# One weight group loaded in four transfers of one row k each, in place of one transfer

## The chip, the cores and the metric

The kernel runs on one core of one Trainium2 chip. The metric is the time of the kernel on the device in microseconds (us), as a median over runs. The profile comes from one execution; its span is counted from the first instruction that the profile shows, so it is a little shorter than the time.

## The reference

The kernel computes a bilinear form for 32 pairs of vectors and 128 weight matrices:

```python
batch, dim_i, dim_j, dim_k = 32, 256, 256, 128
x: [batch, dim_i] float32
y: [batch, dim_j] float32
weight: [dim_k, dim_i, dim_j] float32       # 33.6 MB

out[b, k] = sum over i, j of x[b, i] * y[b, j] * weight[k, i, j]
```

The weight is nearly all of the data. Each row k of it is a matrix of 256 x 256 float32, which is 256 KiB in one piece.

## The kernel before

The 128 rows k are taken in 32 groups of 4 rows: group g holds k = g, g+32, g+64 and g+96. On chip, partition p = 4 * ip + kk holds eight neighbouring i (i = 8 * ip to 8 * ip + 7) of row k = 32 * kk + g, so each partition receives 8 KiB of contiguous weight per group. The PE multiplies a group by a matrix that holds x in the right places, adding up over the eight i, and the DVE multiplies the sums by y and adds over j.

Thirty of the groups are brought in by transfers on the Pool queue, which turn float32 into bf16 on the way. The first two groups to be issued (0 and 16) are brought in as float32 by the SP and ACT queues, and ACT turns them into bf16 with copies. These are the parts concerned:

```python
UNITS = (                         # groups that share a stretch of PE and DVE work
    tuple(range(0, 32, 2)), tuple(range(1, 32, 4)), (3, 11, 19, 27), (7, 23), (15,), (31,),
)
LOADS = (                         # transfers on the Pool queue: groups, from ic, to ic
    ((8, 24), 0, 8), ((4, 12, 20, 28), 0, 8), (tuple(range(2, 32, 4)), 0, 8),
    (tuple(range(1, 32, 4)), 0, 8), ((3, 11, 19, 27), 0, 8), ((7, 23), 0, 8), ((15,), 0, 8),
    ((31,), 0, 4), ((31,), 4, 6), ((31,), 6, 7), ((31,), 7, 8),
)
FIRST = (0, 16)                   # the two float32 groups
# ...
    def rows_of(groups):
        step = G // len(groups)
        v = weight.rearrange("(u s) (ip ic) j -> s ip u (ic j)", s=step, ic=IC)
        return v[groups[0]]       # one group: 32 ip x 4 kk x 2048 elements
# ...
    w_sb = sbuf("w_sb", [P, G, IC * J], bf16)
    w_f = sbuf("w_f", [P, len(FIRST), IC * J], f32)
# ...
    sw = [nc.gpsimd.dma_start(out=w_of(groups)[:, :, lo * J:hi * J],
                              in_=rows_of(groups)[:, :, lo * J:hi * J]).then_inc(s, 16).ins
          for (groups, lo, hi), s in zip(LOADS, s_w)]
    # ... the load of y is put in as the third of these
    hw = [nc.scalar.dma_start(out=x_sb, in_=x).then_inc(s_x, 16).ins]
    for n, (g, queue) in enumerate(zip(FIRST, (nc.sync, nc.scalar))):
        hw.append(queue.dma_start(
            out=w_f[:, n:n + 1, :], in_=rows_of((g,)),
        ).then_inc(s_f[n], 16).ins)
    # ... both lists are moved ahead of the barrier that starts the program
    for n, g in enumerate(FIRST):
        for h in range(2):
            lo, hi = h * IC * J // 2, (h + 1) * IC * J // 2
            c = act.copy(out=w_sb[:, place_of[g], lo:hi], in_=w_f[:, n, lo:hi])
            if h == 0:
                c._wait_ge(s_f[n], 16)
            c.then_inc(s_act, 1)
# ...
    pe.wait_ge(s_act, 2 * len(FIRST))
    pe.wait_ge(s_dve, t_x)
    # ... then per unit: products (each waits for its load), DVE multiply and sum
    sp.dma_start(out=out_v, in_=acc)._wait_ge(s_dve, n_dve).then_inc(s_out, 16)
```

Of the kernel before, what the change touches and what calls it, by code (L numbers as in the profile page):

```python
# [31 lines left out]
FIRST = (0, 16)  # L32
# [4 lines left out]
def kernel(  # L37
# [7 lines left out]
    nc = tc.nc  # L45
# [10 lines left out]
    KK = P // B  # L56
    IP = P // KK
    IC = I // IP
    G = K // KK
# [6 lines left out]
    def sbuf(name, shape, dtype):  # L66
        return nc.alloc_sbuf_tensor(name, shape, dtype).ap()

    def rows_of(groups):


        step = G // len(groups)
        assert all(g == groups[0] + n * step for n, g in enumerate(groups))
        v = weight.rearrange("(u s) (ip ic) j -> s ip u (ic j)", s=step, ic=IC)
        return v[groups[0]]

    def w_of(groups):
        at = [place_of[g] for g in groups]
        step = at[1] - at[0] if len(at) > 1 else 1
        assert all(a == at[0] + n * step for n, a in enumerate(at))  # L80
        return w_sb[:, at[0]:at[-1] + 1:step, :]

    w_sb = sbuf("w_sb", [P, G, IC * J], bf16)
    w_f = sbuf("w_f", [P, len(FIRST), IC * J], f32)
# [18 lines left out]
        for s, (groups, lo, hi) in zip(s_w, LOADS) for g in groups for ic in range(lo, hi)  # L103
    }
    s_f = [nc.alloc_semaphore(f"f{g}") for g in FIRST]
# [15 lines left out]
            out=w_of(groups)[:, :, lo * J:hi * J],  # L121
            in_=rows_of(groups)[:, :, lo * J:hi * J],
# [6 lines left out]
    hw = [  # L129
        nc.scalar.dma_start(out=x_sb, in_=x).then_inc(s_x, 16).ins,  # L130
    ]
    for n, (g, queue) in enumerate(zip(FIRST, (nc.sync, nc.scalar))):
        hw.append(
            queue.dma_start(
                out=w_f[:, n:n + 1, :], in_=rows_of((g,)),
            ).then_inc(s_f[n], 16).ins
        )
    for ins in [*hw, *sw]:
        tc.no_tile_sem_insts.add(ins.name)

# [8 lines left out]
    for blk in blocks:  # L149
# [20 lines left out]
        out=ident, in_=ident, compare_op=mybir.AluOpType.not_equal, fill=1.0,  # L170
# [4 lines left out]
    for n, g in enumerate(FIRST):  # L175
        for h in range(2):
            lo, hi = h * IC * J // 2, (h + 1) * IC * J // 2
            c = act.copy(out=w_sb[:, place_of[g], lo:hi], in_=w_f[:, n, lo:hi])  # L178
            if h == 0:
                c._wait_ge(s_f[n], 16)  # L180
            c.then_inc(s_act, 1)


# [2 lines left out]
    def done(ins):  # L186
# [6 lines left out]
        out=x_rep,  # L193
        in_=x_sb.rearrange("b (ip ic) -> b ic ip", ic=IC).unsqueeze(3)
        .to_broadcast([B, IC, IP, KK]),
    )._wait_ge(s_x, 16))
    for q in range(Q):
        c = v.transpose(  # L198
            out=xt[q * 32:(q + 1) * 32, :, :],
            in_=x_rep[:, :, q * IP // Q:(q + 1) * IP // Q, :],  # L200
        )
# [4 lines left out]
        out=mask, in_=ident.rearrange("p (ip kk) -> p kk ip", kk=KK), axis=AX, op=add,  # L206
    )._wait_ge(s_pool, 2))

    for kk in range(KK):
        c = v.tensor_scalar(  # L210
            out=xblk[:, :, :, kk], in0=xt, scalar1=mask[:, kk:kk + 1],
            scalar2=None, op0=mult,
        )
# [6 lines left out]
        out=yt, in_=y_sb.rearrange("b (jb j) -> b jb j", j=32),  # L220
    )._wait_ge(s_y, 16))
    t = done(v.tensor_copy(  # L222
        out=y_rep, in_=yt.unsqueeze(3).to_broadcast([B, J // 32, B, KK]),
    )._wait_ge(s_dve, t))
    BQ = B // Q
    for q in range(Q):
        c = v.transpose(  # L227
            out=y4[q * 32:(q + 1) * 32, :].rearrange("p (jb j) -> p jb j", j=32),
            in_=y_rep[:, :, q * BQ:(q + 1) * BQ, :],
        )  # L230
# [5 lines left out]
    def product(out, lhsT, rhs, first, last, load):  # L236
        return pe.add_instruction(mybir.InstMatmult(  # L237
            name=nc.get_next_instruction_name(), engine=mybir.EngineType.PE,
            ins=[pe.lower_ap(rhs), pe.lower_ap(lhsT)], outs=[pe.lower_ap(out)],
            start_tensor_calc=first, stop_tensor_calc=last,  # L240
            tile_size=(P, P), tile_position=(0, 0), ldweights=load,
        ))
# [9 lines left out]
    for u, unit in enumerate(UNITS):  # L252
# [13 lines left out]
        for n_step, (ic, h) in enumerate(steps):  # L266
            n = n_g // n_b
# [7 lines left out]
            for s in need[:-1]:  # L275
                pe.wait_ge(s, 16)
            c = product(
                ps[:, bank + h, :n, :],
                xblk[:, ic, :, :].rearrange("p b kk -> p (b kk)"),
                w_sb[:, p0 + o:p0 + o + n, ic * J:(ic + 1) * J],  # L280
                first=(ic == order[0]), last=(ic == order[-1]), load=(held != ic),
            )
# [10 lines left out]
        if n_g > 1:  # L293
            t = done(v.tensor_tensor(  # L294
                out=prod, in0=sums, in1=y4.unsqueeze(1).to_broadcast([P, n_g, J]), op=mult,
# [3 lines left out]
                out=acc[:, unit[0]:unit[-1] + 1:unit[1] - unit[0]], in_=prod, axis=AX, op=add,  # L299
            )._wait_ge(s_dve, t))  # L300
        else:
            done(v.tensor_tensor_reduce(  # L302
                out=prod[:, 0, :], in0=sums[:, 0, :], in1=y4, scale=1.0, scalar=0.0,
# [44 lines left out]
```

## Time and profile before

| | |
|---|---|
| time, median of 3 runs | 84.87 us (84.86 to 84.88) |
| span of the profile | 83.4 us |
| PE busy | 32.5 us (39%) |
| DVE busy | 25.2 us (30%) |
| Pool busy | 8.8 us (11%) |
| ACT busy | 5.2 us (6%) |
| read from HBM | 33.62 MB |
| Pool queue's transfers, share of the 16 DMA engines' span | 94.4% |
| the two other queues' transfers | 3.5% and 3.3% |

The shares of the engines are averages over the whole span. A low share says only that an engine has idle time, not that it is free when it matters. The profile shows the DMA both as issues (an instruction on SP, ACT or Pool that starts a transfer) and as the packets that the 16 DMA engines then move; an issue ends long before its data has landed. The page counts moved bytes as they are written, so a transfer that turns float32 into bf16 counts half of what it reads.

### The profile page before, as it was taken

To read this page: it belongs to the slowest core of one execution; us is meant where nothing else is said; L and a number is where in the kernel's file an instruction comes from. 1 tells how busy PE (TensorE), PEld (TensorE's weight loads), DVE (VectorE), ACT (ScalarE), POOL (GpSimd) and SP (SyncE) were. 2 spreads that over 40 slices of the span, in tenths; PEclk is the share of its full clock that TensorE was granted. 3 is DMA by queue.
4 is the path that set the end of the run, shared out by engine and by line. 5 is a ranking of instruction groups with operands and counts; after the bars stand their busy time and mean duration, and the time that the engine had idled before them with its cause. 6 is when DMAs were issued, how large, how long until landed. Compare 5 with 4: busy or idle time off the path is not lost.

```text
span 83.4 us, 257 instructions
## 1 busy us (share of the span) xinstructions
PE 32.5 (39%) x136; PEld 4.3 (5%) x43; DVE 25.2 (30%) x28; ACT 5.2 (6%) x5; POOL 8.8 (11%) x18
## 2 busy tenths in 40 slices
PE   0000000000000000000099999996029999884780
PEld 0000000000000000000000000000000110112330
DVE  0009450000292000000000000003999800999932
ACT  0019930000000000000000000000000000000000
POOL 5999600000000000000000000000000000000000
PEclk9999999999999999999999999999995799999998
DMA  4999999999999999999999999999999999999980
GB/s 122 393 370 293 214 214 212 216 218 212 218 218 216 212 216 216 212 218 214 212 214 218 210 220 214 214 214 216 212 214 218 212 214 216 212 216 214 197 118 8
DMA packets 4912, 17.91 MB, mean 215 GB/s; under 512 B 384, under 2 KB 800, under 8 KB 4656
## 3 DMA queue, kind: packets, MB, share of 16 engines
q0 software_dynamic: 4432, 15.76, 94.4%
q1 hardware_dynamic: 288, 1.07, 3.5%
q10 hardware_dynamic: 192, 1.08, 3.3%
HBM read 33.62 MB, written 0.02 MB: 403 GB/s over the span
## 4 chain that ended last, share of the span: by engine, by line
DMA 46%; PE 39%; DVE 6%; POOL 3%; another core or an unknown queue 3%; issue 2%; POOLq 0%
DMA w_sb<-in_weight_dram 46%; PE ps L237 39%; DVE tmp L294 5%; POOL w_sb L120 2%; POOL y_sb L127 1%; DVE tmp L302 1%; POOL const-float32-0.0 L332 0%; POOLq L332 0%; POOL const-uint8-127 L332 0%; POOL const-float32-1.0 L332 0%; DVE acc L302 0%
## 5 line engine op out<-in xcount | busy, mean ns | idle before, releaser
L237 PE MATMUL ps<-w_sb,xblk 128*128 128x512 bf16 (+1 forms) x136 | 32.5, 396 | 48.9 <-DMA w_sb<-in_weight_dram 44.2
L294 DVE TENSOR_TENSOR tmp<-ps,y 128x4096 f32<-128x4096 f32 (+3 forms) x4 | 8.6, 2156 | 36.7 <-PE ps L237 36.6
L298 DVE TENSOR_REDUCE acc<-tmp 128x16 f32<-128x4096 f32 (+3 forms) x4 | 8.6, 2154 | 0.1
L237 PEld LDWEIGHTS ps<-w_sb,xblk 128*128 128x128 bf16 x43 | 4.3, 101 | 76.9 <-DMA w_sb<-in_weight_dram 42.7
L120 POOL DMA_DIRECT2D w_sb<-in_weight_dram x11 | 7.6, 707 | 0.6 <-issue 0.6
L178 ACT CAST w_sb<-w_f 128x1024 bf16<-128x1024 f32 x4 | 3.9, 1040 | 0.0
L219 DVE STREAM_TRANSPOSE yt<-y_sb 32x256 f32<-32x256 f32 x1 | 0.4, 433 | 10.9 <-DMA y_sb<-in_y_dram 10.9
L192 DVE COPY x_rep<-x_sb 32x1024 f32<-32x1024 f32 x1 | 0.8, 790 | 6.1 <-PEq L332 6.1
L227 DVE STREAM_TRANSPOSE y<-y_rep 32x256 f32<-32x256 f32 x4 | 1.7, 435 | 0.1
L198 DVE STREAM_TRANSPOSE xt<-x_rep 32x256 f32<-32x256 f32 x4 | 1.7, 435 | 0.1
L178 ACT ACT_TABLE_LOAD x1 | 1.3, 1283 | 6.0 <-PEq L332 6.0
L210 DVE TENSOR_SCALAR xblk<-xt,mask 128x256 bf16<-128x256 f32 x4 | 1.4, 499 | 0.0
L302 DVE CUSTOM_DVE_ANT_0 tmp<-ps,y 128x256 f32<-128x256 f32 x2 | 0.8, 424 | 1.6 <-PE ps L237 1.6
L222 DVE COPY y_rep<-yt 32x1024 f32<-32x1024 f32 x1 | 0.7, 682 | 0.0
L205 DVE TENSOR_REDUCE mask<-ident 128x4 f32<-128x128 f32 x1 | 0.4, 382 | 1.0 <-POOL ident L169 1.0
L127 POOL DMA_DIRECT2D y_sb<-in_y_dram x1 | 0.5, 534 | 0.0
L168 POOL MEMSET ident<- 128x128 f32 x1 | 0.3, 302 | 0.0
L169 POOL TENSOR_SCALAR_AFFINE_SELECT ident<-ident 128x128 f32<-128x128 f32 x1 | 0.3, 287 | 0.1
L302 DVE DVE_READ_ACCUMULATOR2_ANT acc<- 128x1 f32 x2 | 0.2, 84 | 0.0
L332 POOL MEMSET const-float32-0.0<- 128x1 f32 x1 | 0.1, 98 | 0.2 <-issue 0.2
L332 POOL MEMSET const-bfloat16-1.0<- 128x1 bf16 x1 | 0.1, 101 | 0.0
L332 POOL MEMSET const-uint8-127<- 128x1 uint8 x1 | 0.1, 101 | 0.0
(1 smaller groups left out, 0.1 us busy)
## 6 DMA issues: line engine op xcount, KB each, us to landing
w_sb<-in_weight_dram POOLq DMA_DIRECT2D x2, 4096.0 KB, 48.0
w_sb<-in_weight_dram POOLq DMA_DIRECT2D x2, 2048.0 KB, 43.3
w_sb<-in_weight_dram POOLq DMA_DIRECT2D x2, 1024.0 KB, 40.9
w_f<-in_weight_dram SPq DMA_DIRECT2D x1, 1024.0 KB, 4.9
w_f<-in_weight_dram ACTq DMA_DIRECT2D x1, 1024.0 KB, 8.3
w_sb<-in_weight_dram POOLq DMA_DIRECT2D x1, 512.0 KB, 72.1
w_sb<-in_weight_dram POOLq DMA_DIRECT2D x1, 256.0 KB, 72.7
w_sb<-in_weight_dram POOLq DMA_DIRECT2D x1, 128.0 KB, 72.9
```

Source lines behind the costliest of these rows:

```text
L120: nc.gpsimd.dma_start(out=w_of(groups)[:, :, lo * J:hi * J], in_=rows_of(groups)[:, :, lo * J:hi * J],).then_inc(s, 16).ins
L127: sw.insert(2, nc.gpsimd.dma_start(out=y_sb, in_=y).then_inc(s_y, 16).ins)
L178: c = act.copy(out=w_sb[:, place_of[g], lo:hi], in_=w_f[:, n, lo:hi])
L192: t = done(v.tensor_copy(out=x_rep, in_=x_sb.rearrange("b (ip ic) -> b ic ip", ic=IC).unsqueeze(3) .to_broadcast([B, IC, IP, KK]),)._wait_ ...
L198: c = v.transpose(out=xt[q * 32:(q + 1) * 32, :, :], in_=x_rep[:, :, q * IP // Q:(q + 1) * IP // Q, :],)
L210: c = v.tensor_scalar(out=xblk[:, :, :, kk], in0=xt, scalar1=mask[:, kk:kk + 1], scalar2=None, op0=mult,)
L222: t = done(v.tensor_copy(out=y_rep, in_=yt.unsqueeze(3).to_broadcast([B, J // 32, B, KK]),)._wait_ge(s_dve, t))
L227: c = v.transpose(out=y4[q * 32:(q + 1) * 32, :].rearrange("p (jb j) -> p jb j", j=32), in_=y_rep[:, :, q * BQ:(q + 1) * BQ, :],)
L237: return pe.add_instruction(mybir.InstMatmult(name=nc.get_next_instruction_name(), engine=mybir.EngineType.PE, ins=[pe.lower_ap(rhs), pe.l ...
L294: t = done(v.tensor_tensor(out=prod, in0=sums, in1=y4.unsqueeze(1).to_broadcast([P, n_g, J]), op=mult,)._wait_ge(s_pe, n_pe))
L298: done(v.tensor_reduce(out=acc[:, unit[0]:unit[-1] + 1:unit[1] - unit[0]], in_=prod, axis=AX, op=add,)._wait_ge(s_dve, t))
L302: done(v.tensor_tensor_reduce(out=prod[:, 0, :], in0=sums[:, 0, :], in1=y4, scale=1.0, scalar=0.0, op0=mult, op1=add, accum_out=acc[:, uni ...
```

## The change

Group 0, the first float32 group, was one transfer on the SP queue that fills all 128 partitions, with four 8 KiB pieces that lie 8 MiB apart in the weight following each other. It becomes four transfers on the same queue, one for each row k. Each of them reads one row k, 256 contiguous KiB, and writes it to 32 partitions that are four apart (kk, kk+4, ...). All four count on the same semaphore, so the first copy on ACT waits for 64 instead of 16. Group 16, on the ACT queue, stays one transfer. The aim is that a short transfer can begin to move data sooner than a long one, and that each transfer reads the weight in one piece. The contents of `w_f` are the same.

```diff
-    for n, (g, queue) in enumerate(zip(FIRST, (nc.sync, nc.scalar))):
+
+    for kk in range(KK):
         hw.append(
-            queue.dma_start(
-                out=w_f[:, n:n + 1, :], in_=rows_of((g,)),
-            ).then_inc(s_f[n], 16).ins
+            nc.sync.dma_start(
+                out=w_f[kk::KK, 0, :],
+                in_=weight[kk * G + FIRST[0]].rearrange("(ip ic) j -> ip (ic j)", ic=IC),
+            ).then_inc(s_f[0], 16).ins
         )
+    hw.append(
+        nc.scalar.dma_start(
+            out=w_f[:, 1:2, :], in_=rows_of(FIRST[1:]),
+        ).then_inc(s_f[1], 16).ins
+    )
...
-                c._wait_ge(s_f[n], 16)
+                c._wait_ge(s_f[n], 16 if n else 16 * KK)
```

## The prediction

> **What bounds the kernel now.** I read the slices of the page first, then the waits of the PE, then the last stretch of the timeline, and last the start of the timeline, because only the start is touched by the change.
>
> The slices show which resource is full over the whole span. The two DMA rows of the page are:
>
> ```profile
> DMA  4999999999999999999999999999999999999980
> GB/s 122 393 370 293 214 214 212 216 218 212 218 218 216 212 216 216 212 218 214 212 214 218 210 220 214 214 214 216 212 214 218 212 214 216 212 216 214 197 118 8
> ```
>
> From the second slice to the 38th (2.1 to some 79 us) the 16 DMA engines are never idle. The rate row has two levels. Near 400 GB/s the float32 groups move (8 KiB read, 8 KiB written). Near 214 GB/s the groups that are turned into bf16 on the way move (8 KiB read, 4 KiB written); the page counts the written bytes, so the read rate there is also about 430 GB/s. The page's HBM line gives 33.62 MB read. The stream is one unbroken queue of reads.
>
> The waits of the PE (engine, line, what it waited for: us in total, times, longest) show who is ahead of whom:
>
> ```profile
> PE ps L237 <- DMA w_sb<-in_weight_dram: 44.2, 5, 41.9
> PE ps L237 <- DVE tmp L294: 4.6, 1, 4.6
> ```
>
> The PE starts its first product only at 41.87 us, when the load of 8 groups has come in. The 4.6 us behind the DVE lie at 57.5 to 62.1 us and are made good later, as the end of the timeline shows (start us, us, engine, line, what; idle before, and who ended it):
>
> ```profile
> 76.09 1.89 PE L237 MATMUL ps<-w_sb,xblk 128*128 128x512 bf16 x8 [1.32 <-DMA w_sb<-in_weight_dram]
> ...
> 78.51 1.03 PE L237 MATMUL ps<-w_sb,xblk 128*128 128x256 bf16 x8 [0.53 <-DMA w_sb<-in_weight_dram]
> ...
> 79.76 1.64 PE L237 MATMUL ps<-w_sb,xblk 128*128 128x256 bf16 x8 [0.22 <-DMA w_sb<-in_weight_dram]
> ...
> 81.44 0.42 DVE L302 CUSTOM_DVE_ANT_0 tmp<-ps,y 128x256 f32<-128x256 f32 x1 [1.42 <-PE ps L237]
> ...
> 81.90 0.35 SPq L311 DMA_DIRECT2D out_dram<-acc  x1
> ```
>
> Each of the last units waits for its load. By the trace's landing times the last load is complete at 81.07 us; one product (0.3), one product-and-sum on the DVE (0.42) and the output transfer follow, to 83.4. So the end is: start of the DMA stream, plus the time that the busiest of the 16 engines needs for its share, plus a fixed tail of 2.3 us. Only the first two can move.
>
> The start of the timeline, for the three transfers that begin the stream and the one that follows them on the Pool queue:
>
> ```profile
> 0.00 0.63 SPq L134 DMA_DIRECT2D w_f<-in_weight_dram  x1
> 0.12 0.42 ACTq L130 DMA_DIRECT2D x_sb<-in_x_dram  x1
> ...
> 0.58 0.56 ACTq L134 DMA_DIRECT2D w_f<-in_weight_dram  x1
> 1.05 1.60 POOL L120 DMA_DIRECT2D w_sb<-in_weight_dram  x2 [0.61 <-issue]
> ...
> 7.33 3.88 ACT L178 CAST w_sb<-w_f 128x1024 bf16<-128x1024 f32 x4
> ```
>
> Two things count. The issue of 128 rows took 0.63 us, that of 32 rows (x) 0.42. And the copies of the first float32 group begin at 7.33 us, while that group landed 4.9 us after its issue (page, DMA issues): ACT is held by the barrier (6.04 us) and its table load (1.28 us), not by this transfer.
>
> From the trace's packet records I take three more numbers. The first packet of x starts at 1.16 us, 1.04 us after its issue. The first packet of the first group starts at 1.42 us, 1.42 us after its issue, though issued earlier. A packet of 8 KiB takes 309 ns (26.5 GB/s per engine), except in the first round, where it takes 0.4 to 0.6 us. The group runs to 4.57 us; the second float32 group starts at 4.19 us, when the first one drains, and the casting loads from 5.48 us. No engine has a gap between these.
>
> [...] all three queues together move some 400 GB/s at the start, as one stream[...]. [...] the trace shows x (32 rows) with 16 completions. [...] No run of this case shows port contention so far. [...]
>
> **The change part by part.** Removed: one issue on SP of 128 rows by 8 KiB (0.63 us). Added: four issues on SP of 32 rows by 8 KiB. The wait of the first ACT copy goes from 16 to 64 counts, all of them needed, so it still means that all four rows k are in. Nothing else moves: the order of instructions on PE, DVE, ACT and Pool is the same.
>
> Bytes: 1 MiB before and after, 128 packets of 8 KiB, 8 per engine. Data time is 8 x 0.309 = 2.47 us per engine in both. Completions: four per engine instead of one, of 9 ns each (size of the four-byte packets in the trace), so 3 x 9 = 27 ns more per engine. On the path: +0.03 us.
>
> SP's time: by x's 0.42 us per 32-row issue and some 0.04 us between, 4 x 0.46 = 1.84 us instead of 0.63. SP then waits for the barrier until 5.96 us, which Pool releases at 5.92 us. There are 4 us of slack, so this costs nothing.
>
> Feeding: a piece of 256 KiB occupies the engines for 2 x 0.309 = 0.62 us, and the next one is issued 0.46 us later (0.67 us if each costs as much as 128 rows did). The first round is slow (0.5 to 0.6 us), which gives some 0.25 us of lead, and from about 2 us the second float32 group, issued by ACT at 0.58 us, can fill a gap. I count no gap.
>
> Start: if a 32-row transfer starts as soon after issue as x did, the stream starts at 1.04 instead of 1.42 us, up to 0.38 us earlier. Whether the 0.38 us depends on the number of rows is not shown, as x's start may also be quick for another reason (its rows are 1 KiB). I take half of it: -0.2 us. It passes to the end in full, because the engines are never idle afterwards.
>
> ACT copies: the ACT group may now slip in between the second and third piece, which puts the landing of the first group at 6 to 8 us instead of 4.9. The copies would begin perhaps 1 us after 7.33 us. They end at 11.2 us, and the PE has its first work at 41.87 us: some 30 us of slack, no cost.
>
> Sum: -0.2 + 0.03 = about -0.17 us without contention, 84.7 us.
>
> **The rivals.** First, write ports. [...] a piece could take up to twice its 0.62 us: 4 x 0.62 = 2.5 us more in the worst case, 87.2 us. [...] Against it: the starts of the engines are staggered by up to 0.26 us, which takes part of the conflict away; the second group and then the casting loads mix in[...]. I give a full conflict 6%, a partial one (+0.4 to +1.5 us) 15%.
>
> Second, the start gains nothing or the pieces leave gaps. The wait before 1.42 us may be a fixed cost of the first issue on SP, and each piece may bring its own start, with the slow first round paid again in part. For it: first-round packets cost up to 0.3 us above the later ones. That gives 0 to +0.5 us, 84.9 to 85.4. I give it 30%.
>
> Third, all of the start is gained, and 256 contiguous KiB are also read with a quicker first round. The group took 4.57 - 1.42 = 3.15 us where 2.47 are pure data, so up to 0.5 us could be had: 84.2 to 84.4. Against it: from the second round on the packets are already at 309 ns. 15%.
>
> Fourth, the issue time on SP delays the barrier. It would need SP to be busy past 5.9 us, three times what I count, and even then the DMA stream would not notice. No cost.
>
> **Range and chances.** The centre lies between the sum without contention (84.7) and the rival of ports and gaps, so 84.75 us. Below, 84.3 holds the gain of the whole start and a little of the first round. Above, 85.7 holds the gaps and a mild conflict. A gain of 2% is 1.7 us, more than the whole time from the first issue to the first packet (1.42 us); 1% for it. A loss of 2% (above 86.57 us) needs a nearly full port conflict: 7%. Within 2%: 92%.
>
> **What would show each step right or wrong.** In the profile after: four SP issues of 0.4 to 0.5 us each, done before 2 us; DMA busy by 1.1 to 1.3 us; the second slice at 390 GB/s or more; the last units still waiting on their loads, shifted by the same amount as the first landing of the casting loads (12.45 us before); the PE's first product at about 41.7 us. A second or third slice well below 370 GB/s with packets of the first group longer than 0.4 us would show the port conflict; a hole in the DMA share between 2 and 4 us would show gaps. I am wrong in kind if the shift of the end differs from that of the casting stream, since then something other than the start of the stream moved.

## The result, and the profile after

The changed kernel takes 87.17 us (86.49 to 87.67, six executions) against 84.85 us before: a ratio of 1.0276, with a 95% interval of 1.0232 to 1.032. It is slower by 2.3 us, where the prediction had 84.75 us and a range that ended at 85.7. A ratio in this document leaves out every execution more than 1.5% above the fastest of its kernel.

The order of reading is that of the prediction. First the two DMA rows of the page after, in 40 slices of 2.1 us:

```profile
DMA  3999999999999999999999999999999999999800
GB/s 119 351 326 296 231 216 220 216 216 214 217 215 216 214 218 218 216 214 216 214 214 221 214 216 214 214 216 214 214 216 214 214 218 212 216 214 200 132 10 8
```

The second and third slices moved 351 and 326 GB/s, where the kernel before had 393 and 370; the fourth, with 296, is no lower than before (293). The casting loads (those on the Pool queue that turn float32 into bf16) keep their 214 GB/s; there is only more of them at the end. The loss lies in the first 6 us.

The waits of the PE (engine, line, what it waited for: us in total, times, longest) and the end of the timeline say the same from the other side:

```profile
PE ps L244 <- DMA w_sb<-in_weight_dram: 46.8, 5, 44.3
PE ps L244 <- DVE tmp L301: 4.6, 1, 4.6
```

```profile
83.89 0.42 DVE L309 CUSTOM_DVE_ANT_0 tmp<-ps,y 128x256 f32<-128x256 f32 x1 [1.41 <-PE ps L244]
84.24 0.08 DVE L309 DVE_READ_ACCUMULATOR2_ANT acc<- 128x1 f32 x1
84.35 0.35 SPq L318 DMA_DIRECT2D out_dram<-acc  x1
```

The PE starts at 44.3 us instead of 41.9. The wait behind the DVE is the same 4.6 us, and the last product-and-sum starts at 83.89 instead of 81.44. What waits for a complete load is later by 2.4 us from first to last.

The issues of the changed kernel on SP and ACT (start, us, engine, line, what):

```profile
0.00 2.44 SPq L135 DMA_DIRECT2D w_f<-in_weight_dram  x4
```

```profile
0.12 0.40 ACTq L130 DMA_DIRECT2D x_sb<-in_x_dram  x1
0.56 0.71 ACTq L141 DMA_DIRECT2D w_f<-in_weight_dram  x1
```

Four issues of 256 KiB take 2.44 us, about 0.61 us each with the gap, where one issue of 1 MiB took 0.63. A quarter of the rows costs nearly the full issue. And a piece keeps the engines busy for 2 x 0.309 = 0.62 us. So the pieces are issued just as fast as they are moved, and I infer that no store of work builds up in front of the engines.

The stretches from 2 to 4 us show what that does. The last two columns are the share of DMA time in which a packet was under way, and the rate. Before and after:

```profile
2.00:3.00 1.00, 0.00 (x0) 0.00 (x0) 0.00 (x0) 0.00 (x0) 1.00 (x2) 1.00 1.04 426
3.00:4.00 1.00, 0.00 (x0) 0.00 (x0) 0.00 (x0) 0.00 (x0) 1.00 (x2) 1.00 0.99 401
```

```profile
2.00:3.00 1.00, 0.00 (x0) 0.00 (x0) 0.00 (x0) 0.00 (x0) 1.00 (x2) 1.00 0.91 279
3.00:4.00 1.00, 0.00 (x0) 0.00 (x0) 0.00 (x0) 0.00 (x0) 1.00 (x2) 1.00 0.96 385
```

The share falls little, the rate from 426 to 279 GB/s. So the engines are not only idle; some packets also take longer. In the trace's packet records of the changed kernel, seven of the second piece's first packets take 578 to 742 ns in place of 309. Two of the seven (694 and 731 ns) came to an engine that had been empty for some 0.5 us, the other five followed directly on the packet before. One engine is hit hardest. The records carry no engine number, but packets of one engine follow each other to within 20 ns, so its row can be put together:

```
start us   what                           took ns
2.41       group 0 (SP), 8 KiB            578
2.98       group 0 (SP), 8 KiB            332
3.31       completion of the second piece
           (nothing for 0.85 us)
4.17       group 16 (ACT), 8 KiB          1909
6.07       casting load (Pool)            489
```

The other fifteen engines got their first packet of group 16 between 3.07 and 3.55 us. This one got it at 4.17 us, empty by then, and the packet took 1.9 us. It has done one packet in 2.8 us where its neighbours did eight or nine. The trace has 16 landings for each transfer (304 for the 19 of this run), by the order of the packets one per engine. The PE goes on after the last of them: the last load's last landing is at 83.53 us, and the weight load for the product that waits for it starts at 83.57. So the slowest engine decides. The 16 landings of the last load, from the trace:

| last load lands, us | first engine | mean | second to last | last |
|---|---|---|---|---|
| before | 80.59 | 80.81 | 81.01 | 81.07 |
| after | 80.89 | 81.33 | 81.94 | 83.53 |

The last engine is 2.46 us later, which is the whole loss. The mean engine is 0.52 us later; the other 1.94 us are how much further the slowest engine falls behind the mean. It never gets them back: the 16 landings of the casting loads keep this spread from the first load to the last. The first casting load shows the same straggler (one engine far behind the rest) at 12 to 15 us (last landing 14.91 us, second to last 13.32; before 12.45 and 12.40).

### The profile page after: what moved, and what is told of

It is laid out like the page before. It is cut to its first block, busy times and chain, and to the rows that moved or that the text cites. A ratio compares the mean times of both kernels' runs of the same rounds, so it can differ in the third digit from the quotient of the medians.

```text
span 85.8 us, 260 instructions
## 1 busy us (share of the span) xinstructions
PE 32.3 (38%) x136; PEld 4.3 (5%) x43; DVE 25.2 (29%) x28; ACT 5.2 (6%) x5; POOL 8.8 (10%) x18
## 4 chain that ended last, share of the span: by engine, by line
DMA 48%; PE 38%; DVE 6%; another core or an unknown queue 3%; POOL 3%; issue 1%; POOLq 0%
DMA w_sb<-in_weight_dram 48%; PE ps L244 38%; DVE tmp L301 5%; POOL w_sb L120 2%; POOL y_sb L127 1%; DVE tmp L309 0%; POOL const-float32-0.0 L339 0%; POOLq L339 0%; POOL const-uint8-127 L339 0%; POOL const-float32-1.0 L339 0%; DVE acc L309 0%
```

## The experiments

My first theory after the result was that ACT's transfer of group 16, which goes between the second and third piece, holds an engine up. Its rivals were the write side (in pieces of 32 partitions the engines collide where they write) and the read side (256 contiguous KiB are a bad spread over the memory). Both were assumptions; no trace had shown either. From the fifth run on it is the theory of a lead. By it, a transfer that moves for longer than it takes to issue (a whole group: 2.47 us against 0.63) gives time to issue the next ones ahead, and this lead keeps the engines supplied; where issue and movement take equally long (a piece: 0.61 and 0.62 us) there is no lead, and any delay leaves engines empty.

**All on one queue.** SP issues the four pieces and then group 16; ACT issues only x.

```diff
-        nc.scalar.dma_start(
+        nc.sync.dma_start(
             out=w_f[:, 1:2, :], in_=rows_of(FIRST[1:]),
```

> Group 16 is issued by SP after the four pieces instead of by ACT, so only one queue carries float32 weight and no transfer can come between the pieces. Two queues theory (the ACT transfer goes between the second and third piece, and one of the 16 engines is held up by that): no straggler among the 16 completions of a casting load (last behind second last by under 0.2 us, after: 1.6 us), 84.9 us +- 0.3. Partition theory (pieces of 32 partitions make engines collide at the write side): the loss stays, 86.5 to 87.5 us. Contiguity theory (256 KiB read in one piece is a poor spread over the memory): the loss stays, 86.5 to 87.5 us.

Measured: 87.06 us (86.56 to 88.07, four executions), ratio 1.0238 (1.0189 to 1.0286). The straggler is gone (last load's landings 81.80 to 82.97, last behind second to last 0.23 us), but the mean engine is now 1.4 us late. So the second queue is not needed for the loss. In its trace nine of the 16 engines have no packet for 0.3 to 0.8 us just after 3.1 us, and the first packets after that take up to some 1 us.

**Four pieces over all partitions.** Each piece has 128 partitions and 2 KiB of each row.

```diff
-                out=w_f[kk::KK, 0, :],
-                in_=weight[kk * G + FIRST[0]].rearrange("(ip ic) j -> ip (ic j)", ic=IC),
+                out=w_f[:, 0:1, kk * IC * J // KK:(kk + 1) * IC * J // KK],
+                in_=rows_of(FIRST[:1])[:, :, kk * IC * J // KK:(kk + 1) * IC * J // KK],
```

> Four pieces on SP again and ACT as in the changed kernel, but each piece fills all 128 partitions with 2 KiB each, in place of 32 partitions with 8 KiB. Two queues theory: the ACT transfer still comes between the pieces, the straggler stays, 86.5 to 87.5 us. Partition theory: no loss, 84.9 to 85.2 us [...]. Contiguity theory: each piece reads from four rows k again, no loss, 84.9 to 85.2 us.

Measured: 87.39 us, ratio 1.0299 (1.0282 to 1.0316). Neither the four-apart partitions nor the contiguous 256 KiB are left in it, and a loss of the same size is. But it is not the same loss in detail: from 2 to 3 us this run moves only 129 GB/s, in packets of 2 KiB, and all its engines are late (the mean by 1.85 us, the last 0.15 us behind the second to last). So this run weighs against both rivals without refuting them.

**The pieces behind a whole transfer, on ACT.** Group 0 is whole on SP, group 16 comes in four pieces of one row k on ACT.

```diff
+    hw.append(
+        nc.sync.dma_start(
+            out=w_f[:, 0:1, :], in_=rows_of(FIRST[:1]),
+        ).then_inc(s_f[0], 16).ins
+    )
     for kk in range(KK):
         hw.append(
-            nc.sync.dma_start(
-                out=w_f[kk::KK, 0, :],
-                in_=weight[kk * G + FIRST[0]].rearrange("(ip ic) j -> ip (ic j)", ic=IC),
+            nc.scalar.dma_start(
+                out=w_f[kk::KK, 1, :],
+                in_=weight[kk * G + FIRST[1]].rearrange("(ip ic) j -> ip (ic j)", ic=IC),
```

> Group 0 is one transfer on SP as before the change, and group 16 on ACT is the one in four pieces of one row k. SP has a single transfer, so nothing can come between the pieces from the other float32 queue. Two queues theory: 84.9 us +- 0.3, no straggler. Partition theory and contiguity theory: the same four pieces cost what they cost in the changed kernel, 86.5 to 87.5 us, perhaps less as the casting loads mix in.

Measured: 85.44 us, ratio 1.0065 (1.0044 to 1.0085). The same kind of pieces costs 0.56 us here and not 2.3. They are moved from 4.4 us on, behind 2.5 us of data that was already queued.

**Quadrants.** Each piece goes to 32 neighbouring partitions.

```diff
+                out=w_f[kk * 32:(kk + 1) * 32, 0:1, :],
+                in_=rows_of(FIRST[:1])[kk * IP // Q:(kk + 1) * IP // Q],
```

> Four pieces on SP and ACT as in the changed kernel, but each piece goes to 32 neighbouring partitions, and reads 64 KiB from each of four rows k. Two queues theory: the straggler stays, 86.5 to 87.5 us. Partition theory: worse than the changed kernel[...]: 87 to 90 us, packets of the pieces at 0.6 us. Contiguity theory: the read is spread again, 84.9 us +- 0.3.

Measured: 87.56 us, ratio 1.0308 (1.0288 to 1.0329), but with a picture that none of the theories had. The trace shows the engines in two halves: eight engines' last load lands at 79.71 to 80.16 us and the other eight's at 83.63 to 83.93. The source pattern of a piece now starts with a dimension of 8; that this is the cause is not shown. The run cannot decide about the write side. It shows by itself how an uneven start passes to the end. My estimate, which takes it that eight engines moved all 128 packets of the pieces (not shown engine by engine): eight packets more on each of these at 309 ns are 2.5 us, and the last load lands 2.86 us later than before.

**Two pieces instead of four.** Two rows k each, 64 partitions two apart.

```diff
-    for kk in range(KK):
+    for kk in range(2):
...
-                out=w_f[kk::KK, 0, :],
-                in_=weight[kk * G + FIRST[0]].rearrange("(ip ic) j -> ip (ic j)", ic=IC),
+                out=w_f[kk::2, 0:1, :],
+                in_=rows_of(FIRST[:1])[:, kk::2, :],
```

> Group 0 on SP in two pieces of two rows k each (64 partitions, two apart) instead of four; ACT as in the changed kernel. Lead theory (a piece of 256 KiB takes about as long to issue, 0.6 us, as to move, [...] and each hiccup leaves engines empty): an issue of some 0.65 us now covers 1.24 us of data, so a lead builds up after the first piece; most of the loss is gone, 84.9 to 85.4 us. Boundary theory (each of the three boundaries costs the same): one third of 2.3 us stays, 85.5 to 85.8 us. Partition theory: 64 partitions two apart[...], 86 to 87.5 us.

Measured: 85.13 us, ratio 1.0025 (1.0009 to 1.0041). An issue of 0.6 us now stands against 1.24 us of data. The loss is not a third of 2.3 us, as equal boundaries would have it, but a tenth. That is the median: the 20 executions lie between 84.87 and 86.64 us, three of them above 85.8, so two pieces can still lose much.

**Whole first, pieces second, one queue.** Group 0 whole, then group 16 in the four pieces, all on SP: the first run with the order turned round.

> SP issues group 0 whole and then group 16 in four pieces, all on one queue; ACT issues only x. It is the single-queue run with the order turned round. Lead theory: the pieces come behind a transfer that moves for 2.5 us while they are issued, so engines do not run empty: 85.0 to 85.6 us. Boundary theory: same number of pieces as in the single-queue run, same loss, 86.5 to 87.5 us.

Measured: 85.15 us, ratio 1.0037 (1.0013 to 1.0061). The timeline of SP in this run:

```profile
0.00 0.65 SPq L134 DMA_DIRECT2D w_f<-in_weight_dram  x1
0.70 1.86 SPq L140 DMA_DIRECT2D w_f<-in_weight_dram  x3
```

The pieces are issued at the same pace as in the changed kernel (the three that this line merges in 1.86 us), each still reads its 256 contiguous KiB into 32 partitions four apart, and they cost 0.3 us. In the single-queue run four pieces and one whole group in the other order cost about 2 us. So it is the order that counts; the lead is the theory that had forecast this.

**The pieces alone, and their reference.** Group 16 goes to the Pool queue, so SP has the only float32 weight; then the same with group 0 whole.

```diff
 LOADS = (
+    ((16,), 0, 8),
...
-FIRST = (0, 16)
+FIRST = (0,)
```

> Group 16 goes to the Pool queue as one more casting load, so SP's four pieces are the only float32 weight; ACT issues only x. To be read against the next run. Lead theory: engines run empty between the pieces (DMA share below 0.95 somewhere between 2 and 4 us) and the loss against the next run is 0.5 to 2 us. Second-queue theory (the loss needs ACT's transfer between the pieces): loss below 0.3 us.

> As the run before, with group 0 as one transfer: the reference for it. Both theories: no empty engines between 2 and 4 us as long as the Pool queue delivers by then (its first packet came at 5.5 us in the kernel before, at 3.4 us at the earliest seen); 84.8 to 85.6 us.

Measured: 86.88 us with pieces (ratio to the kernel before 1.0225, 1.0182 to 1.0267) and 85.41 us whole (1.006, 1.0031 to 1.0089). The pieces cost 1.5 us with no second float32 transfer at all, inside the range of the lead theory. The stretches of the run with pieces, columns as above:

```profile
2.00:3.00 1.00, 0.00 (x0) 0.00 (x0) 0.00 (x0) 0.00 (x0) 1.00 (x3) 1.00 1.05 426
3.00:4.00 1.00, 0.00 (x0) 0.00 (x0) 0.00 (x0) 0.00 (x0) 1.00 (x2) 1.00 0.92 217
```

The first two pieces move at 426 GB/s. The 217 GB/s from 3 to 4 us are not an empty stream: on fourteen engines casting packets follow the second piece from 3.12 us on without a gap, and the casting loads write at 214 GB/s. But two engines have nothing from 3.13 and 3.15 us to 4.51 and 4.55 us, which fits the share of 0.92, and their next packets take 1.54 and 1.58 us in place of 0.32. These two end 1.9 us behind the rest (last load 83.34 and 83.41 us, the others up to 81.46). The mean engine lands the last load at 81.54 us here and at 81.56 us with group 0 whole, so the whole difference lies in these two.

Two things in this pair do not come out of the lead theory. With group 0 whole, eleven of the first casting packets took 0.8 to 1.8 us, and each followed directly on the packet before: a packet can be as long as that at the start of a transfer without an empty engine. And with the pieces, the third and fourth were issued by 1.81 and 2.44 us, but their first packet comes at 4.67 us, while two engines stood empty. The time of the issue alone does not account for that.

**Two issuers.** SP and ACT issue the pieces in turn.

```diff
-            nc.sync.dma_start(
+            (nc.scalar if kk % 2 else nc.sync).dma_start(
                 out=w_f[kk::KK, 0, :],
```

> The four pieces of the changed kernel are issued in turn by SP (rows 0 and 2) and ACT (rows 1 and 3), so each queue needs half as many issues; x first and group 16 last on ACT. Lead theory, if the 0.6 us of an issue is the queue's own: all pieces are issued by 1.3 us instead of 2.4 us, [...] 84.9 to 85.6 us. Lead theory, [...]: issues that overlap each take longer (0.7 us and more), nothing is gained, 86.3 to 87.5 us.

Measured: 86.41 us, ratio 1.0181 (1.0132 to 1.023). The issues in this run, SP and then ACT:

```profile
0.00 1.17 SPq L135 DMA_DIRECT2D w_f<-in_weight_dram  x2
```

```profile
0.56 1.52 ACTq L135 DMA_DIRECT2D w_f<-in_weight_dram  x2
2.11 0.62 ACTq L141 DMA_DIRECT2D w_f<-in_weight_dram  x1
```

ACT's two issues take 0.70 and 0.79 us beside SP's 0.54 and 0.58, and the last piece is issued by 2.08 us, not by 1.3. So two queues do not double the pace. Whether that is because they share something is not shown: ACT's issue of 0.79 us began at 1.30 us, when SP was done (1.17 us), and ACT's four pieces behind a whole transfer took 0.52 to 0.69 us, so ACT may only be the slower of the two. Group 16 came later for it, at 2.11 us, and after 3.7 us fifteen engines took a casting packet of 1.1 to 2.0 us. The run fits the second form of the lead theory, at the lower end of what it expected.

**ACT's group first.** The changed kernel with ACT's two transfers swapped: group 16 at 0.12 us, x behind it.

```diff
-    hw = [
-        nc.scalar.dma_start(out=x_sb, in_=x).then_inc(s_x, 16).ins,
-    ]
+    hw = []
... (the four pieces on SP, group 16 on ACT)
+    hw.append(nc.scalar.dma_start(out=x_sb, in_=x).then_inc(s_x, 16).ins)
```

> The changed kernel with ACT's two transfers swapped: group 16 (2.5 us of data) is issued at 0.1 us, before x, so it stands behind the first piece and pieces two to four stand behind it. The pieces themselves are as in the changed kernel. Lead theory: the engines have a full queue from the second transfer on, most of the loss is gone, 84.8 to 85.6 us, no engine 1 us behind the others. Boundary theory (every piece costs its own 0.6 to 0.8 us): 86.5 to 87.5 us.

Measured: 84.91 us, ratio 1.0013 (1.0006 to 1.002). The pieces are as in the changed kernel, and the loss is gone. ACT's issues, and the stretches:

```profile
0.12 0.60 ACTq L139 DMA_DIRECT2D w_f<-in_weight_dram  x1
0.76 0.67 ACTq L143 DMA_DIRECT2D x_sb<-in_x_dram  x1
```

```profile
2.00:3.00 1.00, 0.00 (x0) 0.00 (x0) 0.00 (x0) 0.00 (x0) 1.00 (x2) 1.00 0.96 401
3.00:4.00 1.00, 0.00 (x0) 0.00 (x0) 0.00 (x0) 0.00 (x0) 1.00 (x2) 1.00 1.03 418
```

From 2 us the rate is 401 and 418 GB/s, as in the kernel before. Group 16 stands behind the first piece with 2.5 us of data, and pieces two to four are issued long before it ends. None of the pieces' 128 packets takes more than 364 ns, and the first piece had the engines to itself. Had the engines been in each other's way at the write ports, as the prediction's first rival assumes, some packets should have taken up to twice 309 ns. The last load lands between 80.83 and 81.41 us, without a straggler.

**The changed kernel again**, unaltered: once for a second trace, then in many executions.

> The changed kernel once more, unaltered, for a second trace. If the straggling engine comes from running empty, some engine (one to three of 16) again shows a hole in its packets between 3 and 5 us, followed by a packet of over 1 us, and its last casting load lands 1 us or more after the others: 86.5 to 87.7 us. If the 1.9 us packet of the first trace was chance, no such packet, with the time still near 87.

Two executions: 86.73 us (the traced one) and 84.86. In the trace three engines have the hole, 0.8 to 1.1 us long, from 3.1 or 3.2 us on. Their first packets of group 16 start at 4.04, 4.10 and 4.22 us and take 1.13, 1.18 and 1.58 us, and these three land the last load at 82.85 to 83.10 us, the other thirteen by 81.85. The 84.86 was not expected, and led to the next run.

> The changed kernel unaltered, in five rounds beside the kernel before. Lead theory (whether an engine runs empty is decided in each execution [...]): a spread of more than 1 us between executions, some near 85 us where no engine ran empty, most between 86 and 87.7 us, median 86 to 87.3 us. A fixed cost of the pieces would give a spread like that of the kernel before, 0.4 us, around 87.2 us.

24 executions: median 86.89, from 84.75 to 88.1 us. Seven lie between 84.75 and 85.68, seventeen between 86.47 and 88.1, none between; the 27 of the kernel before lie between 84.6 and 84.97. The ratio for this series, 1.003 (1.0012 to 1.0049), is that of the seven lower ones alone, so the list has to be read instead. The traced execution (87.11 us) has four engines with the late start, landing at 83.17 to 83.51, the rest by 81.61. So the loss is not a fixed cost of four pieces. It falls or does not fall in each execution. No execution of the lower kind was traced, so that none of its engines ran empty is inferred.

**The kernel before, with x behind group 16.**

> The kernel before with ACT's two transfers swapped (group 16 before x), to see whether a full queue from the start gains anything. Lead theory: the engines were never empty after 1.7 us in the kernel before, so at most the 0.1 us that x's packets take at the head of the stream: 84.6 to 84.9 us.

Measured: 84.94 us, ratio 1.0011 (1.0002 to 1.002), just above the expected range. There is nothing to gain at the head of the stream in this way. No version that I ran is faster than the kernel before.

## Why the prediction was wrong

**What held.** The bound: the DMA stream, then a fixed tail of 2.3 us. The first casting load lands 2.46 us later (12.45 to 14.91), and so does the last (81.07 to 83.53): the prediction had said that the two shifts must agree. The start of the stream: the first packet of group 0 comes at 1.32 us instead of 1.42, so 0.1 us were gained where I took 0.2 of a possible 0.38. The order: group 16 did go between the second and third piece (it starts at 3.07 us, the third piece at 5.62). The copies on ACT start later, at 11.2 us and not at the 8 I had, and it costs nothing, since the PE begins at 44.3. SP's four issues end at 2.44 us instead of 1.84, still far from the barrier at 5.9.

**The step that failed** is "Feeding", with its last sentence "I count no gap". It had both numbers side by side, 0.62 us of data per piece and 0.46 to 0.67 us per issue. Measured is 0.61 us per issue: I took x's 0.42 us as the price of a 32-row issue, but a 32-row issue of weight costs 0.54 to 0.59 us plus a gap. Nor is 0.42 us a fixed price of x: where x came behind group 16 on ACT, its issue took 0.67 us (the swap) and 0.75 us (the kernel before with x behind). With 0.61 us, supply and demand are equal. I then argued that the slow first round gives 0.25 us of lead and that group 16 would fill what is missing. What the runs showed in its place: two engines stood empty for some 0.5 us ahead of the second piece, and group 16 reached a third 0.85 us late. The two runs on one queue (about 87 us with the pieces first, 85.15 with the whole group first) and the swap on ACT (84.91 us) show that the same four pieces lose this time only where no large transfer stands ahead of most of them. The lead is the explanation that forecast these runs; that it is the whole mechanism is not shown.

**The second term that was mis-sized** is the price of a gap. The second rival named gaps and a second slow start, and gave them 0 to 0.5 us. For the mean engine that is right: 0.52 us. But I priced the average. The end is set by the slowest of the 16, and the packet behind the gap took 1.9 us, not 0.6. The gap of 0.85 us and the 1.60 us that this packet took beyond 309 ns are 2.45 us on one engine, and that is the result.

**The first rival**, a full conflict of write ports, had put 87.2 us to its name. The number agrees and the cause does not: the same 32 partitions four apart run at 307 to 364 ns per packet in the swap on ACT, and cost 0.3 us behind a whole transfer. The sign that I had set for it did appear (a third slice of 326 GB/s, packets of the first group of up to 742 ns), and it misled: late and slow first packets give the same sign. For these pieces no such conflict was seen in the swap, with no packet above 364 ns. That write ports can bind, and the factor of two that I took for it, were assumptions of the prediction; no trace of this case shows them.

**The range** was too narrow for that reason. A loss of over 2% was tied to the port conflict alone and got 7%; the gaps, which were the more likely rival at 30%, were not allowed to reach it.

Four things stay open: whether the two queues share a part of the issue; why a transfer's first packet reaches one engine so much later than the others; why pieces that have been issued can wait for more than 2 us while an engine is empty (the run with the pieces alone); and why first packets of a transfer take 0.3 us in some cases and 1 to 2 us in others, on engines that were empty and on engines that were not.

## What to carry to other kernels

When the DMA stream is the bound, compare the issue time of a transfer with the time that its data keeps the engines busy. Where the two were equal at the head of the stream (0.61 and 0.62 us), this kernel lost some 2 us in most executions. Put the large transfers first and any small pieces behind them: behind a whole group the same pieces cost 0.3 and 0.56 us here, and with one behind the first piece 0.1 us. And judge a start by its slowest engine, from the spread of the 16 landings, not by the mean rate: here the engine that was 1.59 us behind the next at the first casting load was still 1.59 us behind it at the last, and the kernel ended with it.

## What the runs showed of the hardware that I had not expected

- An issue on SP of 32 rows of 8 KiB took 0.53 to 0.67 us and one of 128 rows 0.60 to 0.65 us. A quarter of the rows took nearly the same time. (One issue of 32 rows in the single-queue run took 1.09 us, and the four of the quadrants took 2.99 us together.)
- ACT's issue of group 16 took 0.71 us beside the pieces on SP, in all three traces of the changed kernel, against 0.56 us in the kernel before.
- Packets at the start of a transfer can take far longer than the 0.31 to 0.32 us of the later ones: up to 1.9 us on an engine that had been empty (the changed kernel), and 0.8 to 1.8 us on engines without a gap (group 0 whole and group 16 cast). An empty engine does not always make them long: the first piece in the swap on ACT met empty engines and took 0.31 to 0.36 us per packet.
- The engines do not get a transfer's first packet at the same time: in the changed kernel group 16 reached fifteen of them within 0.5 us, and the sixteenth 0.6 us after these.
- The time of one and the same kernel can fall in two groups, 84.75 to 85.68 and 86.47 to 88.1 us, without any difference in the granted clock of the PE (0.96 to 0.98 in both).
